# Attention in a decoder trunk: output products of four units in one block, their neighbours' work dealt to three slots of four, and a third PSUM bank for turned exponentials

## The chip, the cores and the metric

The program runs on one core of a Trainium2 chip. The metric is the device time of one execution in microseconds; the kernel before takes 1901.03 us (median of three runs, 1900.66 to 1902.24). TensorE is PE (its weight loads are PEld), VectorE is DVE, ScalarE is ACT, GpSimd is POOL; SP issues most transfers.

## The reference

The trunk has four feed-forward layers (SwiGLU), one short convolution and one attention layer, on 512 tokens of width 1024. Only the attention layer is touched. It is sparse attention in three branches that share 16 heads in 4 groups; with 512 tokens, 8 blocks to select from and 16 selected, the selected branch reads every key, and the window of 512 does so too. Cut to what matters:

```python
s = einsum(q, k) * scale + rel_bias[bucket(dist)]     # per head; k of the selected or of the window branch
p = masked_softmax(s, dist >= 0)
o_branch = einsum(p, v)
out = g0 * o_compressed + g1 * o_selected + g2 * o_window
y = out @ w_out                                       # o is (512, 1024): 16 heads of 64
```

The compressed branch has the same form with 31 compressed keys.

## The kernel before

All large products are in fp32r with operands split into a high and a low part (three matmuls for one, lines 167 to 169). Attention is done by *units*: one unit is one head of one branch with 512 keys (32 units: 4 groups, in each two pairs of heads, in each pair branch 0 for both heads and then branch 1 for both). A unit's work has four stages:

- **logits** (L1277, tile s): eight matmuls in three pieces c = 0, 1, 2, each into a PSUM bank of the tag "s". DVE adds the bias table and takes the smallest (L1287), ACT takes exponentials with their sum (L1296).
- **scaled** (L1302 to L1307): DVE takes reciprocals of the sums, POOL multiplies the unit's exponentials by gate over sum, four instructions.
- **turn** (L1316, tile pt): ten transposes on PE, in three pieces, each into a bank of the tag "t"; ACT copies pieces 0 and 2 to SBUF, DVE piece 1 (L1321, L1322).
- **apply** (L1336, tile o): the turned exponentials times the values, for two heads at once, one into the upper and one into the lower 64 partitions of one bank. The second branch's call adds the compressed branch (L1341, tile o<-pcp,vz), and then ACT and DVE split the finished bank into ohi and olo (L163, L164).

A loop runs over slots v. Slot v issues the logits of unit v+3, scales unit v+2, turns unit v+1, and in every odd slot, behind the third piece, applies units v-1 and v; I call one such call a *block*. Around them a slot takes *pieces* of other work (fill): projections of the next group's queries (twelve matmuls a piece, tile nat, L167 to L169), turning of its heads and keys (tile pk, L1164, followed by DVE at L1182 and L1191), the compressed branch's logits (tile pc, L1231, with DVE at L1235 and L1238, and pct), and the output projection of finished groups (tile y). `share` deals a list of steps to slots by weights; `places` fixes others to a slot. The eight PSUM banks are four pairs: "nat" for nat, pc, pct, pk and y alike, "s" for logits, "t" for turned pieces and "o" for outputs; a pair's banks are taken in turn, in the order of the program text.

The order on each engine is fixed when the program is built: a scheduler takes the instructions by readiness and by the order of the program text, with `issue_after` as a constraint, and each engine then works through its list in that order.

Of the kernel before, what the change touches and what calls it, by code (L numbers as in the profile page):

```python
# [13 lines left out]
F32 = mybir.dt.float32  # L14
F32R = mybir.dt.float32r
# [7 lines left out]
P = 128  # L23
D = 1024
T = 512
# [28 lines left out]
def decoder_kernel(ctx, tc, xT, cT, ng, adaw, adab, ffi, ffo, cwi, cw, cwo,  # L54
# [3 lines left out]
    def pool(es, name, bufs, **kw):  # L58
        kw.setdefault("reuse_waits", "tile")
        return es.enter_context(tc.tile_pool(name=name, bufs=bufs, **kw))  # L60
# [8 lines left out]
    tp = pool(ctx, "tp", 1)  # L69
# [3 lines left out]
    ps = pool(ctx, "ps", 1, space=PSUM)  # L73
    six = cycle(("nat", "s", "t"))


    def psum(name, tag="mm"):
        tag = next(six) if tag == "mm" else {"pr": "o"}.get(tag, tag)
        return ps.tile([P, T], F32, name=name, tag=tag, bufs=2)


    TAGS = {"t": (4, T), "sq": (2, T), "xr": (2, HT), "dg": (1, T)}
# [32 lines left out]


    cbs = [psum("cb", "nat") for c in range(D // T)]
    for c, o in enumerate(cbs):
        nc.tensor.matmul(o, ones[0:1], crow[:, c * T:(c + 1) * T], start=True, stop=True)
# [42 lines left out]
    def split(src, hi, lo):  # L162
        act = nc.scalar.activation(hi, src, AF.Copy)  # L163
        return act, nc.vector.tensor_tensor(lo, src, hi, ALU.subtract)  # L164
# [735 lines left out]
    def nsa(s, nrm, nxt, w0, ahead):  # L900
        with ExitStack() as es:
            na = pool(es, "na", 1, side="right")
            hpool = es.enter_context(ExitStack())
# [11 lines left out]
            kn = [[t[:, :, b] for t in kt] for b in range(2)]  # L915
            vn = [[na.tile([P, NG, HD], F32, name=f"vn{b}{t}") for t in range(NB)] for b in range(2)]
            kc = na.tile([P, NG, 2, NPAD], F32R, name="kc")
            vcc = na.tile([P, HD], F32, name="vcc")
            gsb = na.tile([P, NB, 48], F32, name="gsb")
# [51 lines left out]
            def values_and_gates(dst, own):  # L971
                n = CW + 48
                w = [weights(nwv[:, k:min(k + 3, KD)], min(3, KD - k), n, own if k == 3 else None, 2 if k == 3 else 3)
                     for k in range(0, KD, 3)]
                ge = tmp("ge", NB * 48).rearrange("p (a b) -> p a b", a=NB)

                def quarter(t):
                    o = psum("nat")
                    tk = slice(t * P, (t + 1) * P)
                    for k in range(KD):  # L980
                        wh, wl = w[k // 3]
                        mm3(o[:, 0:n], h[0][k][:, tk], h[1][k][:, tk], wh[:, k % 3, :], wl[:, k % 3, :], k == 0, k == KD - 1)
                    nc.vector.tensor_copy(dst[t], o[:, 0:CW].rearrange("p (g e) -> p g e", e=HD))
                    nc.scalar.activation(ge[:, t, :], o[:, CW:n], AF.Exp, scale=-1.0)
                    if t == NB - 1:
                        nc.vector.tensor_scalar(ge, ge, 1.0, None, op0=ALU.add)
                        nc.vector.reciprocal(gsb, ge)

                return quarter
# [41 lines left out]
            K = [[na.tile([P, T], F32R, name=f"k{b}{e}") for e in range(2)] for b in range(2)]  # L1031
            Q = [na.tile([P, T], F32R, name=f"q{q}") for q in range(NG)]
            keys, spread_keys, heads = turners(qn, kt, K, Q)
# [5 lines left out]
            with ExitStack() as es2:  # L1039
# [21 lines left out]
                v1 = values_and_gates(vn[1], nw)  # L1061
# [8 lines left out]
                v1(3)  # L1070
                for b in range(2):
                    spread_keys(b)
            return attend(es, s, nxt, ahead, K, Q, keys, spread_keys, heads, vn, kc, vcc, gsb, query_steps, value_steps, last_weight, hpool)


    def compressor(es, os, kc, vcc):
# [118 lines left out]

    LOFF = {3: 0, 2: 512, 0: 896, 1: 1024}

    def attend(nsa_es, s, nxt, ahead, K, Q, keys, spread_keys, heads, vn, kc, vcc, gsb, query_steps, value_steps, last_weight, hpool):
        oh, ol = [], []
        ow = pool(nsa_es, "ow", 8, side="right")  # L1200
        units = [(g, 2 * pr + e, b) for g in range(NG) for pr in range(2) for b in range(2) for e in range(2)]
        half = [slice(0, HD), slice(HD, P)]
        with ExitStack() as es:
            at = pool(es, "at", 1)
# [60 lines left out]
            Ls, sts, pts, os, last_turn, last_out = {}, {}, {}, {}, [], []  # L1265
# [43 lines left out]
            def turn(u, c):  # L1309
                pt = psum("pt", "t")  # L1310
                off, segs = 0, []
                for j in ((0,), (1, 3), (2,))[c]:
                    segs.append((j, off))
                    for i in range(j, NB):
                        cc = LOFF[i] + j * P
                        last_turn[:] = [nc.tensor.transpose(pt[:, off:off + P], Ls[u][:, cc:cc + P], ident)]  # L1316
                        off += P
                p = at.tile([P, off], F32, name=f"p{c}", bufs=3)
                pts[u, c] = p, segs
                if c == 1:  # L1320
                    return lambda: nc.vector.tensor_copy(p, pt[:, 0:off])  # L1321
                nc.scalar.activation(p, pt[:, 0:off], AF.Copy)  # L1322
                return lambda: None

            def apply(u):

                g, q, b = units[u]
                if b == 0:
                    os[g, q // 2] = psum("o", "o")
                o = os[g, q // 2]  # L1330
                for c in range(3):
                    both = [pts.pop((u + e, c)) for e in range(2)]
                    for j, cc in both[0][1]:
                        n = T - j * P
                        for e in range(2):
                            last = nc.tensor.matmul(o[half[e], j * P:T], vn[b][j][:, g], both[e][0][:, cc:cc + n],  # L1336
                                                    start=(b == 0 and j == 0), stop=False)
                if b == 0:
                    return last
                for e in range(2):  # L1340
                    last = nc.tensor.matmul(o[half[e]], vz[:, q + e], pcp, start=False, stop=True)  # L1341
                del os[g, q // 2]
                hi, lo = [(tp if g % 2 else ow).tile([P, T], F32R, name=n, tag="t", bufs=4 if g % 2 else 8) for n in ("ohi", "olo")]
                split(o, hi, lo)
                oh.append(hi)
                ol.append(lo)
                return last
# [19 lines left out]
            for g in range(NG):  # L1367
                v0 = 8 * g
# [17 lines left out]
            def share(v):  # L1386
                for steps, n, v0, v1 in shares:
                    if v0 <= v < v1:
                        room = [2 - (i > 0 and i % 2) for i in range(v0, v1)]
                        upto_ = [n * sum(room[:i]) // sum(room) for i in (v - v0, v - v0 + 1)]  # L1390
                        return steps, upto_[1] - upto_[0], v == v1 - 1
                return None, 0, False

            for v in range(START, N):
                a, b, u = v + LEAD, v + 1, v
                steps, n, end = share(v)

                def fill(c):
                    for f in places[v, c]:
                        f()  # L1400
                    for _ in range(n * (c + 1) // 3 - n * c // 3):
                        next(steps, None)

                for c in range(3):
                    if 0 <= a < N:
                        sps = logits(a, c)
                    if c == 0 and 0 <= a - 1 < N:
                        scaled(a - 1)
                    if 0 <= b < N:
                        low = turn(b, c)  # L1410
                    if u % 2 and 0 < u and c == 2:
                        with tc.issue_after(last_turn[0].ins):
                            last_out[:] = [apply(u - 1)]
                    if 0 <= a < N:
                        smallest(a, c, sps)
                    if 0 <= b < N:
                        low()
                    if 0 <= a < N:
                        exponentials(a, c)
                    with tc.issue_after(last_out[0].ins) if last_out and c == 2 else nullcontext():  # L1420
                        fill(c)
                for g, q in tables[v]:
                    table(g, q)
                if end:
                    for _ in steps:
                        pass
        w0 = ahead()
        for a, b in HALVES:
            for d in range(KD):
                o = psum("ty")  # L1430
# [36 lines left out]
    nxt = Norm(1)  # L1467
    soon = upto(1)
    w = ffn(0, 0, nrm, nxt, None, conv_ahead, [small] + late(2, -1), soon)
    nrm, nxt = nxt, Norm(2)  # L1470
# [4 lines left out]
    nrm, nxt = nxt, Norm(3)  # L1475
    w = ffn(2, 1, nrm, nxt, w, ffn_ahead(2), late(5, -3))
    nrm, nxt = nxt, Norm(4)
    w = ffn(3, 2, nrm, nxt, w, lambda: nsa_in(4), late(6))
    cd_es.close()
    nrm, nxt = nxt, Norm(5)  # L1480
    w = nsa(4, nrm, nxt, w, ffn_ahead(3))
    ffn(5, 3, nxt, None, w, None)

# [73 lines left out]
```

## Time and profile before

| what | value |
|---|---|
| median of 3 runs | 1901.03 us |
| the profiled execution's own time | 1900.09 us |
| its span | 1898.3 us |
| PE busy in the span | 1872.5 us, 99% |
| attention slots, first logits to last output product | 1323.9 to 1533.2 us |
| PE, DVE, ACT, POOL busy in these 209.3 us | 203.4, 161.0, 133.8, 80.5 us |

The page of the profile gives busy time by engine, the span in 40 slices, and the chain of work that ended last. The timeline lists instructions of one engine in order with start and duration; "x16" merges sixteen of a kind. A matmul's duration is its latency in the pipeline, so the distance between two starts says what it costs, not the duration. An fp32 product such as o appears twice in the trace (two passes) for one row of the program.

### The profile page before, as it was taken

To read this page: it belongs to the slowest core of one execution; us is meant where nothing else is said; L and a number is where in the kernel's file an instruction comes from. 1 tells how busy PE (TensorE), PEld (TensorE's weight loads), DVE (VectorE), ACT (ScalarE), POOL (GpSimd) and SP (SyncE) were. 2 spreads that over 40 slices of the span, in tenths; PEclk is the share of its full clock that TensorE was granted. 3 is DMA by queue.
4 is the path that set the end of the run, shared out by engine and by line. 5 is a ranking of instruction groups with operands and counts; after the bars stand their busy time and mean duration, and the time that the engine had idled before them with its cause. 6 is when DMAs were issued, how large, how long until landed. Compare 5 with 4: busy or idle time off the path is not lost.

```text
span 1898.3 us, 33954 instructions
## 1 busy us (share of the span) xinstructions
PE 1872.5 (99%) x13293; PEld 1710.8 (90%) x13293; DVE 1562.9 (82%) x2671; ACT 857.5 (45%) x1399; POOL 225.5 (12%) x330
## 2 busy tenths in 40 slices
PE   7999999999999999999999999999999999999999
PEld 5989999988899899999989899999777789898989
DVE  8978888887898888888888888887878778586865
ACT  3434344532245343435634343454666636353432
POOL 0011110000011111100111110000444310010100
PEclk9999999999999999999999999999999999999999
DMA  9587767366756767664667766234333235474731
GB/s 330 176 257 188 244 178 229 116 231 232 254 151 183 229 182 244 180 218 114 172 222 189 225 176 215 70 114 128 87 97 84 69 87 152 140 190 125 187 110 64
DMA packets 126669, 324.60 MB, mean 171 GB/s; under 512 B 16011, under 2 KB 16651, under 8 KB 126508
## 3 DMA queue, kind: packets, MB, share of 16 engines
q1 hardware_dynamic: 95196, 242.72, 37.8%
q0 software_dynamic: 31312, 79.71, 18.5%
q8 instruction: 104, 1.70, 0.4%
q14 instruction: 57, 0.47, 0.1%
HBM read 313.85 MB, written 3.15 MB: 167 GB/s over the span
## 4 chain that ended last, share of the span: by engine, by line
PE 87%; DVE 9%; ACT 2%; issue 1%; DMA 1%; DVEq 0%; ACTq 0%
PE gu L169 13%; PE gu L167 13%; PE gu L168 13%; PE y L167 7%; PE y L169 7%; PE y L168 7%; PE hs L168 2%; PE hs L169 2%; PE hs L167 2%; PE cv L167 2%; PE cv L169 2%; PE cv L168 2%; PE o L1336 2%; PE ty L168 2%; PE ty L169 2%; PE ty L167 2%
## 5 line engine op out<-in xcount | busy, mean ns | idle before, releaser
L163 ACT ACTIVATE whi<-wraw 128x1024 fp32r<-128x1024 f32 (+2 forms) x261 | 254.4, 979 | 370.6 <-PE y L168 205.3
L164 DVE TENSOR_TENSOR wlo<-wraw,whi 128x1024 fp32r<-128x1024 f32 (+2 forms) x261 | 295.2, 1136 | 24.2 <-ACT whi L163 23.2
L167 PE MATMUL y<-ahi,whi 128*128 128x512 f32 x576 | 223.7, 392 | 1.0
L168 PE MATMUL y<-alo,whi 128*128 128x512 f32 x576 | 224.3, 389 | 0.0
L169 PE MATMUL y<-ahi,wlo 128*128 128x512 f32 x576 | 224.2, 389 | 0.0
L147 DVE CUSTOM_DVE_ANT_0 adaraw<-adaraw,cond,adabs 128x1024 f32<-128x1024 f32 x144 | 184.4, 1297 | 27.9 <-DMA adaraw<-in_adaw 27.7
L167 PE MATMUL gu<-hhi,whi 128*128 128x256 f32 x696 | 192.5, 277 | 0.0
L169 PE MATMUL gu<-hhi,wlo 128*128 128x256 f32 x696 | 192.4, 276 | 0.0
L168 PE MATMUL gu<-hlo,whi 128*128 128x256 f32 x696 | 192.4, 276 | 0.0
L655 POOL DMA_DIRECT2D qa<-in_ffi x70 | 84.4, 1206 | 711.7 <-DMA qa<-in_ffi 197.2
L167 PE MATMUL gu<-th,qah 128*128 128x256 f32 x584 | 161.3, 276 | 0.0
L168 PE MATMUL gu<-tl,qah 128*128 128x256 f32 x584 | 161.2, 276 | 0.0
L169 PE MATMUL gu<-th,qal 128*128 128x256 f32 x584 | 161.2, 276 | 0.0
L167 PE MATMUL gu<-th,qbh 128*128 128x256 f32 x584 | 161.2, 276 | 0.0
L168 PE MATMUL gu<-tl,qbh 128*128 128x256 f32 x584 | 161.2, 276 | 0.0
L169 PE MATMUL gu<-th,qbl 128*128 128x256 f32 x584 | 161.2, 276 | 0.0
L167 PEld LDWEIGHTS y<-ahi,whi 128*128 128x128 f32 x576 | 107.2, 188 | 26.9 <-ACT ahi L163 5.7
L167 PEld LDWEIGHTS gu<-hhi,whi 128*128 128x128 f32 x696 | 130.7, 188 | 0.5
L168 PEld LDWEIGHTS gu<-hlo,whi 128*128 128x128 f32 x696 | 130.6, 188 | 0.5
L169 PEld LDWEIGHTS gu<-hhi,wlo 128*128 128x128 f32 x696 | 130.7, 188 | 0.0
L169 PEld LDWEIGHTS y<-ahi,wlo 128*128 128x128 f32 x576 | 108.1, 188 | 22.7
L168 PEld LDWEIGHTS y<-alo,whi 128*128 128x128 f32 x576 | 108.1, 188 | 22.3
(312 smaller groups left out, 5379.6 us busy)
## 6 DMA issues: line engine op xcount, KB each, us to landing
wraw<-in_ffi SPq DMA_DIRECT2D x103, 512.0 KB
adaraw<-in_adaw POOLq DMA_DIRECT2D x79, 512.0 KB, 4.4
qa<-in_ffi SPq DMA_DIRECT2D x146, 256.0 KB
wraw<-in_ffo SPq DMA_DIRECT2D x96, 384.0 KB
qa<-in_ffi POOLq DMA_DIRECT2D x70, 512.0 KB, 6.9
adaraw<-in_adaw SPq DMA_DIRECT2D x65, 512.0 KB
a<-in_ffi SPq DMA_DIRECT2D x73, 256.0 KB
wraw<-in_cwi SPq DMA_DIRECT2D x24, 512.0 KB
```

The source lines that it names most:

```text
L147: return nc.vector.tensor_tensor_reduce(out=raw, in0=raw, in1=cond, scale=scale, scalar=adabs[:, c:c + 1], op0=ALU.mult, op1=ALU.add, accu ...
L163: act = nc.scalar.activation(hi, src, AF.Copy)
L164: return act, nc.vector.tensor_tensor(lo, src, hi, ALU.subtract)
L167: nc.tensor.matmul(o, sh, mh, start=first, stop=False)
L168: nc.tensor.matmul(o, sh, ml, start=False, stop=False)
L169: nc.tensor.matmul(o, sl, mh, start=False, stop=last)
L655: nc.gpsimd.dma_start(qa, bass.AP(tensor=a21.tensor, offset=a21.offset, ap=[a21.ap[0], [0, 2], a21.ap[1]]), accum_op=ALU.add)
L1336: last = nc.tensor.matmul(o[half[e], j * P:T], vn[b][j][:, g], both[e][0][:, cc:cc + n], start=(b == 0 and j == 0), stop=False)
```

## The change

Five things are edited, all in or for `attend`:

- Blocks: in every fourth slot (u % 4 == 3), ahead of piece 1's logits, both branches of a pair of heads are applied one behind the other (`apply(u - 3)`, `apply(u - 1)`), in place of one in every odd slot behind piece 2. Pieces in front of them are constrained by `issue_after` in piece 1 in place of piece 2.
- Dealing: `share` gives weight 1 to the slots without a block and 0 to those with one (before: 2 and 1).
- Banks: within attention the tag "t" rotates over three banks and "o" has one; outside, each tag has two as before.
- Copies: the turned exponentials have 5, 4 and 4 buffers in place of 3 each.
- Room: the pool "ow" has 4 buffers in place of 8; group 2's outputs go to the space of the tiles kn.

```diff
+    banks = {t: cycle((t + "0", t + "1")) for t in ("nat", "s", "t", "o")}
+
     def psum(name, tag="mm"):
         tag = next(six) if tag == "mm" else {"pr": "o"}.get(tag, tag)
-        return ps.tile([P, T], F32, name=name, tag=tag, bufs=2)
+        return ps.tile([P, T], F32, name=name, tag=next(banks[tag]), bufs=1)
...
-        ow = pool(nsa_es, "ow", 8, side="right")
+        ow = pool(nsa_es, "ow", 4, side="right")
+        kept = dict(banks)
+        banks["t"], banks["o"] = cycle(("t0", "t1", "o1")), cycle(("o0",))
...
-                p = at.tile([P, off], F32, name=f"p{c}", bufs=3)
+                p = at.tile([P, off], F32, name=f"p{c}", bufs=(5, 4, 4)[c])
...
-                hi, lo = [(tp if g % 2 else ow).tile([P, T], F32R, name=n, tag="t", bufs=4 if g % 2 else 8) for n in ("ohi", "olo")]
+                if g == 2:
+                    two = na.tile([P, 2, T], F32R, name="o2", tag=f"kn{q // 2}")
+                    hi, lo = two[:, 0], two[:, 1]
+                else:
+                    hi, lo = [(tp if g else ow).tile([P, T], F32R, name=n, tag="t", bufs=4) for n in ("ohi", "olo")]
...
-                        room = [2 - (i > 0 and i % 2) for i in range(v0, v1)]
+                        room = [i < 0 or i % 4 < 3 for i in range(v0, v1)]
...
                 for c in range(3):
+                    if u % 4 == 3 and 0 < u and c == 1:
+                        with tc.issue_after(last_turn[0].ins):
+                            apply(u - 3)
+                            last_out[:] = [apply(u - 1)]
                     if 0 <= a < N:
                         sps = logits(a, c)
                     if c == 0 and 0 <= a - 1 < N:
                         scaled(a - 1)
                     if 0 <= b < N:
                         low = turn(b, c)
-                    if u % 2 and 0 < u and c == 2:
-                        with tc.issue_after(last_turn[0].ins):
-                            last_out[:] = [apply(u - 1)]
...
-                    with tc.issue_after(last_out[0].ins) if last_out and c == 2 else nullcontext():
+                    with tc.issue_after(last_out[0].ins) if last_out and c == 1 else nullcontext():
                         fill(c)
...
+        banks.update(kept)
```

Every engine has the same instructions as before; their order changes between the first logits and the end of attention. (Line numbers of the change are 2 to 10 higher than those of before from line 78 on: L1320 is the transpose L1316, L1340 the product L1336, L1281 the logits L1277, L1166 the transposes of heads and keys L1164, L169 to L171 the three matmuls L167 to L169.)

The first place is PE's list in the opening of attention, where the second group's queries are projected (nat) beside the first units' logits (s) and transposes (pt). Before, a stretch of it:

```order
L1277 MATMUL s<-k_13505,q_13510 128x512
L1277 MATMUL s<-k_13506,q_13510 128x512
L168 MATMUL nat<-wlo,hhi_13485 128x256
L169 MATMUL nat<-whi,hlo_13489 128x256
L167 MATMUL nat<-whi,hhi_13485 128x256
L168 MATMUL nat<-wlo,hhi_13485 128x256
L169 MATMUL nat<-whi,hlo_13489 128x256
L1277 MATMUL s<-k_13505,q_13510 128x384
L1277 MATMUL s<-k_13506,q_13510 128x384
L1277 MATMUL s<-k_13505,q_13510 128x128
```

Of the change, the end of the same stretch:

```order
L1281 MATMUL s<-k_13505,q_13512 128x512
L1281 MATMUL s<-k_13506,q_13512 128x512
L1320 MATMUL pt<-ident,L 128x128 x6
L1281 MATMUL s<-k_13505,q_13512 128x384
L1281 MATMUL s<-k_13506,q_13512 128x384
L1281 MATMUL s<-k_13505,q_13512 128x128
L1281 MATMUL s<-k_13506,q_13512 128x128
L1320 MATMUL pt<-ident,L 128x128 x11
L1340 MATMUL o<-p_14945,vn_13494 64x512
L169 MATMUL nat<-whi,hhi_13484 128x256
L170 MATMUL nat<-wlo,hhi_13484 128x256
L171 MATMUL nat<-whi,hlo_13488 128x256
```

Before, 84 of the 96 matmuls nat of this projection stand between logits and transposes of the first five units, ahead of the first block; now all 96 stand behind the last transpose x11 and the first row of the first block. (The compressed branch's two pieces pc now take both banks of "nat" ahead of this projection, which so waits for DVE's reads at L1235 and L1238; before, the projection's first half had the second bank.)

The second place is PE's list at the end of the first pair of heads, in slot 3. Before, from the last rows of the second block:

```order
L1336 MATMUL o<-p_15161,vn_13500 64x256
L1336 MATMUL o<-p_15263,vn_13500 64x256
L1341 MATMUL o<-pcp,vz 64x512
L1164 MATMUL pk<-ident,qn_14873 128x128 x2
L1164 MATMUL pk<-ident,qn_14874 128x128 x2
L1341 MATMUL o<-pcp,vz 64x512
L1277 MATMUL s<-k_13507,q_13512 128x512
```

And now, from the middle of the one block:

```order
L1340 MATMUL o<-p_15005,vn_13496 64x256
L1340 MATMUL o<-p_15071,vn_13496 64x256
L1340 MATMUL o<-p_15123,vn_13498 64x512
L1340 MATMUL o<-p_15203,vn_13498 64x512
L1340 MATMUL o<-p_15137,vn_13499 64x384
L1340 MATMUL o<-p_15221,vn_13499 64x384
L1340 MATMUL o<-p_15137,vn_13501 64x128
L1340 MATMUL o<-p_15221,vn_13501 64x128
L1340 MATMUL o<-p_15161,vn_13500 64x256
L1340 MATMUL o<-p_15254,vn_13500 64x256
L1345 MATMUL o<-pcp,vz 64x512 x2
L1281 MATMUL s<-k_13507,q_13511 128x384
```

The two branches now follow each other without other rows in between, and nothing stands between the two rows of vz. Over the whole of attention the rows of o stood in 22 runs (16 blocks, of which four were broken up by other rows, two of them into three runs) and stand in 11 now (8 blocks, three of which have their first row alone, ahead of other rows).

More of the change, by code (lines that the diff above doesn't have):

```diff
@@ L1072, in nsa @@
                     spread_keys(b)
-            return attend(es, s, nxt, ahead, K, Q, keys, spread_keys, heads, vn, kc, vcc, gsb, query_steps, value_steps, last_weight, hpool)
+            return attend(es, na, s, nxt, ahead, K, Q, keys, spread_keys, heads, vn, kc, vcc, gsb, query_steps, value_steps, last_weight, hpool)
     def compressor(es, os, kc, vcc):
@@ L1196, in decoder_kernel, with attend @@
     LOFF = {3: 0, 2: 512, 0: 896, 1: 1024}
-    def attend(nsa_es, s, nxt, ahead, K, Q, keys, spread_keys, heads, vn, kc, vcc, gsb, query_steps, value_steps, last_weight, hpool):
+    def attend(nsa_es, na, s, nxt, ahead, K, Q, keys, spread_keys, heads, vn, kc, vcc, gsb, query_steps, value_steps, last_weight, hpool):
         oh, ol = [], []
-        ow = pool(nsa_es, "ow", 8, side="right")
+        ow = pool(nsa_es, "ow", 4, side="right")
+        kept = dict(banks)
+        banks["t"], banks["o"] = cycle(("t0", "t1", "o1")), cycle(("o0",))
         units = [(g, 2 * pr + e, b) for g in range(NG) for pr in range(2) for b in range(2) for e in range(2)]
```

## The prediction

> **What bounds the kernel now.** First the page:
>
> ```profile
> span 1898.3 us, 33954 instructions
> PE 1872.5 (99%) x13293; PEld 1710.8 (90%) x13293; DVE 1562.9 (82%) x2671; ACT 857.5 (45%) x1399; POOL 225.5 (12%) x330
> ...
> PE   7999999999999999999999999999999999999999
> ...
> PE 87%; DVE 9%; ACT 2%; issue 1%; DMA 1%; DVEq 0%; ACTq 0%
> ```
>
> PE is busy in every slice and carries 87% of the chain that ended last, so whatever the change is worth must come out of PE's time in the attention slots (slices 28 to 32 of 40). Behind them PE is as full as ahead of them, so a gain or a loss there reaches the end at its whole size. Then the attention slots, cut where units 2, 6, 10, 14, 18 and 22 begin their logits (columns: length, then busy time of each engine):
>
> ```profile
> 1331.90:1353.70 21.80, 21.12 (x163) 18.00 (x161) 17.03 (x55) 14.66 (x42) 9.46 (x20) 1.00 0.32 87
> 1353.70:1381.00 27.30, 26.33 (x177) 19.37 (x178) 20.81 (x64) 17.90 (x51) 10.95 (x20) 1.00 0.40 104
> 1381.00:1404.00 23.00, 22.52 (x171) 17.99 (x169) 18.10 (x58) 16.00 (x44) 10.00 (x20) 1.00 0.30 86
> 1454.50:1481.40 26.90, 25.22 (x155) 17.86 (x155) 22.61 (x67) 17.64 (x50) 11.88 (x20) 1.00 0.37 85
> sum 209.30, PE 203.37 PEld 155.43 DVE 161.02 ACT 133.78 POOL 80.45; mean PE 22.60 PEld 17.27 DVE 17.89 ACT 14.86 POOL 8.94
> ```
>
> Four units cost 23 us in one stretch and 27 in the next: the long ones turn the next group's heads and keys, where DVE has most to do (20.8 and 22.6 us). PE's idle time in all is only 209.30 - 203.37 = 5.9 us. Who ends it, by the waits of PE in these slots:
>
> ```profile
> PE pt L1316 <- ACT p L1322: 2.2, 4, 0.7
> PE s L1277 <- DVE st L1287: 1.2, 4, 0.3
> PE pt L1316 <- DVE p L1321: 0.5, 1, 0.5
> ```
>
> So 2.7 us are transposes that wait for one of two banks to be copied out. The rest of what can be won is not idle time at all, and the timeline of PE shows it, at two blocks that stand whole:
>
> ```profile
> 1363.55 0.84 PE L1316 MATMUL pt<-ident,L 128*128 128x128 f32 x6
> 1364.14 0.37 PE L167 MATMUL nat<-whi,hhi 128*128 128x256 f32 x1
> ...
> 1396.72 0.48 PE L1277 MATMUL s<-k,q 128*128 128x256 f32 x2
> 1397.04 0.38 PE L1316 MATMUL pt<-ident,L 128*128 128x128 f32 x2
> 1397.35 2.37 PE L1336 MATMUL o<-p,vn 128*64 128x512 f32 x16
> 1399.66 0.39 PE L167 MATMUL nat<-whi,hhi 128*128 128x256 f32 x1
> 1399.88 0.28 PE L168 MATMUL nat<-wlo,hhi 128*128 128x256 f32 x1
> 1400.00 0.28 PE L169 MATMUL nat<-whi,hlo 128*128 128x256 f32 x1
> ...
> 1407.20 2.37 PE L1336 MATMUL o<-p,vn 128*64 128x512 f32 x16
> 1409.40 1.03 PE L1341 MATMUL o<-pcp,vz 128*64 128x512 f32 x4
> 1410.36 0.73 PE L1277 MATMUL s<-k,q 128*128 128x512 f32 x2
> ```
>
> Read the distances between starts. Six transposes take 0.59 us to the next start, 0.10 each; the two ahead of a block take 0.31, so going into it costs 0.11. The block's sixteen passes take 2.31 us where nat follows and 2.20 where its own vz follows: going out costs 0.11, and the first nat behind it takes 0.22 instead of the 0.12 of the next, 0.10 more. **An edge pair costs 0.32 us**, and none of it is counted idle. Blocks that other rows break up are dearer:
>
> ```profile
> 1358.53 1.02 PE L1341 MATMUL o<-pcp,vz 128*64 128x512 f32 x2
> 1359.61 0.44 PE L1164 MATMUL pk<-ident,qn 128*128 128x128 f32 x2
> ...
> 1360.58 1.07 PE L1341 MATMUL o<-pcp,vz 128*64 128x512 f32 x2
> 1361.58 0.73 PE L1277 MATMUL s<-k,q 128*128 128x512 f32 x2
> ...
> 1417.31 1.07 PE L1336 MATMUL o<-p,vn 128*64 128x512 f32 x2
> 1418.31 0.68 PE L1277 MATMUL s<-k,q 128*128 128x512 f32 x2
> ...
> 1420.77 2.37 PE L1336 MATMUL o<-p,vn 128*64 128x512 f32 x14
> 1423.07 0.39 PE L167 MATMUL nat<-whi,hhi 128*128 128x256 f32 x1
> ```
>
> Two rows of vz side by side cost 0.96 us (1409.40 to 1410.36), apart 1.08 + 1.00: **1.1 us more**. A first row of o alone and its fourteen passes later cost 1.00 + 2.30, against 2.31: **1.0 more**. The two heads' rows, in different halves of the array, run side by side only when neighbours.
>
> **The change part by part.** *Edges.* Blocks fall from 16 to 8. One of those saved lies in the opening, which I cost whole below; 7 x 0.32 = -2.2 us.
>
> *Broken blocks.* Before, slots 3 and 13 have the two breaks shown, slots 5 and 21 one each with three runs, taken at 1.1 like the first: 1.1 + 1.0 + 2 x 1.1 = 4.3. Now three blocks have their first row alone, 3 x 1.0 = 3.0. -1.3 us. (Bounds: 0, if a lone row's cost is hidden in a wait, and -2.4, if the three cost a third of that.)
>
> *Alternation.* With pieces gathered in fewer slots, changes from fp32r products (s, nat, y) into transposes fall from 95 to 82. The two s rows at 1396.72 take 0.32 us to the next start where two nat rows take 0.23: at most 0.09 for each change; bounds 0 and -1.2, taken in the middle near nothing, -0.5.
>
> *The opening.* Before, 84 rows of nat fill PE while the first units go through DVE, ACT and POOL; now they come later, and PE waits on that chain. Its pace, by POOL:
>
> ```profile
> 1328.88 0.20 POOL L1304 TENSOR_TENSOR f<-r,gsb 128x4 f32<-128x4 f32 x1 [15.79 <-DVE r L1302]
> 1329.19 2.05 POOL L1307 TENSOR_SCALAR L<-L,f 128x128 f32<-128x128 f32 x4
> 1332.38 0.20 POOL L1304 TENSOR_TENSOR f<-r,gsb 128x4 f32<-128x4 f32 x1 [1.14 <-DVE r L1302]
> ...
> 1342.62 0.28 PE L167 MATMUL nat<-whi,hhi 128*128 128x256 f32 x1
> 1346.26 0.28 PE L169 MATMUL nat<-whi,hlo 128*128 128x256 f32 x1
> ...
> 1353.64 0.73 PE L1277 MATMUL s<-k,q 128*128 128x512 f32 x2 [0.31 <-DVE st L1287]
> ```
>
> The first two units are 3.5 us apart. The transposes x11 need unit 4 scaled: 1328.9 + 4 x 3.3 (a little under 3.5, since no nat stands between) + 2.4 for POOL = 1344.5. Then 96 nat at (1346.26 - 1342.62)/32 = 0.114 make 10.9, four pct 0.4, the first row of o 0.45 without its break: unit 6 begins at 1356.3 instead of 1353.6. By then the change has also done some 0.9 us less of PE's work (seven rows of o fewer, 7/8 of 2.20 = 1.9, against seven transposes and the rest more). Together **+3.6 us**. At a pace of 3.0 (POOL is busy 2.4 a unit, so there is room) it is +2.4, at 3.5 +4.4. The cover, were it there, would be any other PE work ready in that time; the list has none.
>
> *The third bank and the copies.* Transposes no longer wait for the copy of two pieces back: at best the 2.7 us of the waits above go. At worst, logits wait more: their banks are still two, and during a block of 2.20 + 2.20 + 0.96 = 5.4 us no logits come, then all at once. Behind the block in slot 3 stand, on PE, pk and the next logits; on DVE, olo, then L1287, L1191 and L1182 in one list; POOL's scaling waits for those, and the next transposes for POOL. Against that DVE has a projection's normalisation and a weight split to do under the block. Bounds -5.9 (all idle time) and +7.5 (rival C); taken near the row for the transposes, less 0.5 for logits: -2.2.
>
> *Nothing.* `ow`, kn's space and the order of transfers: SP's list differs by a few places, and no wait of PE in the rows above is on a transfer. ACT and POOL have 209.3 - 133.8 and more to spare; what covers them is PE itself.
>
> Sum: -2.2 - 1.3 - 0.5 + 3.6 - 2.2 = **-2.6 us** on the span, 1895.7. The profiled execution took 1900.1 for a span of 1898.3, and the median lies 0.9 above it: 1895.7 + 1.8 + 0.9 = **1898.4 us**.
>
> **The rivals.** *B, the waits go with the edges* (chance 0.20). With PE free of short stalls all 5.9 us of idle time go, and the opening runs at 3.0 a unit: -2.2 - 1.3 - 0.5 + 2.4 - 5.9 = -7.5, 1893.5 us. For it: 2.7 of 5.9 are exactly what a third bank removes. Against: the rest waits for DVE and other banks. [...]
>
> *C, the long block starves DVE* (0.18): slower. A block holds PE 5.4 us at a stretch instead of 2.3 and 3.2, so DVE is without logits for some 2.5 us longer; in the three stretches with heads and keys, where DVE needs 20.8 to 22.6 us and PE's own work is not much more, that time comes back as PE's waits: 3 x 2.5 = +7.5 in place of -2.2. Sum +7.1, 1908.1 us. It decides where the DVE work left at a block's end is longer than PE's up to the next one. For it: L1287 waits for PE already. Against: DVE was idle 6.5 us in 27.3 there, and waits that fall under a block cost nothing. [...] The trace shows so far that the stretch with more DVE work is the longer one, 27 against 23 us.
>
> *D, the gain and the opening cancel* (0.20). The transposes' waits turn into waits for logits, none saved: -0.4 and less, 1900.6 to 1904. The change then does what it says and PE is only idle elsewhere.
>
> **How the numbers follow.** The forecast, 1898.4, has 0.42; its own range is 1895.5 to 1900.5. Bounds of the unknown terms give 1893.5 to 1908; the range that leaves out less than two in ten is 1891.5 to 1906. A measurement of this kernel tells about 0.2%, 3.8 us, from no change: faster means below 1897.2, which takes B and 0.18 of the forecast, 0.38; slower, above 1904.8, is C, 0.18; the rest, 0.44, is no difference.
>
> **What would show it.** Edges: the sum of L1336's time should fall while its count stays; two blocks back to back in 5.4 us. Opening: unit 6's logits about 2.7 us later after the first logits than now, PE idle about 4 us before the first row of nat. Bank: no PE wait of pt for ACT's copy; if those stay, the third bank was not the limit. C would show as PE's waits of s for DVE growing from 1.2 us to several in the stretches of heads and keys. I am wrong about the opening if PE is not idle there, and about the edges if the 27 us stretches do not shrink.

## The result: slower by 0.7%

The changed kernel takes 1914.73 us (median of six, 1913.27 to 1917.77), beside it the kernel before 1900.99: ratio 1.0072, interval 1.0061 to 1.0083. Forecast were 1898.4 us and at most 1906.0. The profiled execution took 1917.77 us, the longest of the six, so its losses are some 3 us above those of the median. Its page:

```profile
span 1916.0 us, 33925 instructions
PE 1879.0 (98%) x13293; PEld 1719.7 (90%) x13293; DVE 1564.9 (82%) x2671; ACT 857.0 (45%) x1399; POOL 223.5 (12%) x330
...
PE 83%; DVE 7%; issue 5%; POOL 2%; ACT 1%; DMA 1%; SPq 0%; DVEq 0%; POOLq 0%; ACTq 0%
```

POOL, with 12% of busy time, is new in the chain that ended last. The span is 17.7 us longer. Of this 1.7 is, in the main, a wait for a weight (y for wlo, 1.6) at 522 us, long ahead of the change (the other traces show none there or up to 0.5 us); 0.9 lies just ahead of the first logits, 0.9 behind attention, and 14.2 in attention itself: 223.2 us from the first logits to the last output product, before 209.0. The stretches that begin with the logits of units 2, 6, 10 and 22, and the sum over attention (columns as before; behind POOL stands the granted clock of TensorE, 1.00 being full speed):

```profile
1334.90:1362.80 27.90, 25.41 (x175) 20.79 (x174) 16.60 (x54) 15.80 (x46) 8.99 (x20) 0.98 0.29 89
1362.80:1390.00 27.20, 24.86 (x169) 20.38 (x167) 22.42 (x66) 18.08 (x49) 9.06 (x20) 0.94 0.42 110
1390.00:1412.90 22.90, 22.61 (x170) 18.42 (x169) 16.81 (x56) 15.62 (x43) 9.18 (x20) 1.00 0.17 42
1465.70:1495.60 29.90, 26.56 (x156) 20.14 (x155) 25.32 (x66) 18.94 (x50) 11.54 (x23) 0.94 0.50 136
...
sum 223.20, PE 209.06 PEld 163.45 DVE 162.51 ACT 134.31 POOL 78.64; mean PE 23.23 PEld 18.16 DVE 18.06 ACT 14.92 POOL 8.74
```

PE's idle time rose from 5.9 to 14.1 us, and its busy time rose by 6.0 with the same instructions. DVE, ACT and POOL have no more to do than before. The opening up to unit 6 takes 36.3 us in place of 29.8; the stretch from 22 to 26 takes 29.9 in place of 26.9.

**Who ends the idle time.** The waits of PE in attention:

```profile
PE pt L1320 <- POOL L L1311: 7.9, 18, 1.2
PE y L169 <- DVE q L1193: 2.0, 1, 2.0
PE s L1281 <- DVE st L1291: 0.9, 4, 0.3
PE pk L1166 <- DVE q L1193: 0.8, 1, 0.8
PE pt L1320 <- DVE p L1325: 0.3, 1, 0.3
```

(Each row: what waited, for whom; us in total, number of waits, the longest.) The waits for ACT's copies are gone, as the third bank was to do. In their place transposes wait for POOL's scaling, 18 times; before, no wait of PE for POOL stood in this list. More of the same hides in PE's busy time: adding the distances from one start to the next over all 320 transposes, without idle time, gives 41.9 us in place of 35.0. They come one or two at a time as POOL finishes a row block, and their weight loads wait for POOL 34 times, before twice:

```profile
PEld pt L1320 <- POOL L L1311: 16.5, 34, 1.3
```

**Where the wait begins.** PE behind the first block, that of slot 3:

```profile
1368.60 0.79 PE L1281 MATMUL s<-k,q 128*128 128x384 f32 x4
...
1373.65 0.66 PE L1166 MATMUL pk<-ident,qn 128*128 128x128 f32 x4 [0.77 <-DVE q L1193]
1374.11 1.11 PE L1281 MATMUL s<-k,q 128*128 128x384 f32 x6
1376.22 1.70 PE L1320 MATMUL pt<-ident,L 128*128 128x128 f32 x4 [1.00 <-POOL L L1311]
...
1379.60 0.56 PE L169 MATMUL nat<-whi,hhi 128*128 128x256 f32 x1
```

DVE in the same time:

```profile
1367.73 1.29 DVE L960 TENSOR_TENSOR qn<-qn,rs_r 128x512 f32<-128x512 f32 x2
1368.94 1.22 DVE L166 TENSOR_TENSOR wlo<-wraw,whi 128x1024 fp32r<-128x1024 f32 x1
1370.07 0.69 DVE L166 TENSOR_TENSOR olo<-o,ohi 128x512 fp32r<-128x512 f32 x1
1370.67 0.55 DVE L1291 CUSTOM_DVE_ANT_0 L<-s,tb 128x384 f32<-128x384 f32 x1
...
1375.25 0.16 DVE L1306 RECIPROCAL r<-st 128x4 f32<-128x4 f32 x1
```

And POOL:

```profile
1365.16 2.09 POOL L1311 TENSOR_SCALAR L<-L,f 128x128 f32<-128x128 f32 x4
1375.49 0.20 POOL L1308 TENSOR_TENSOR f<-r,gsb 128x4 f32<-128x4 f32 x1 [8.24 <-DVE r L1306]
1375.79 2.05 POOL L1311 TENSOR_SCALAR L<-L,f 128x128 f32<-128x128 f32 x4
```

Of before, the same scaling:

```profile
1368.91 0.20 POOL L1304 TENSOR_TENSOR f<-r,gsb 128x4 f32<-128x4 f32 x1 [5.33 <-ACT p L1322]
```

In the change the first logits behind the block come at 1368.6, DVE gets to them at 1370.7, the reciprocals are there at 1375.4, POOL, idle for 8.2 us, begins at 1375.5 and the transposes at 1376.2. That chain is no longer than before: there the logits behind the same products stood at 1361.6 and POOL began at 1368.9, 7.3 us against 6.9. What is missing is PE's work beside it. Before, twenty transposes, twelve nat and the next block's first row, with logits and pk, filled that time; now thirteen transposes, logits and pk stand there, the block has run whole ahead of it, and the first nat comes at 1379.6.

**The clock.** PE's other loss is one that the prediction doesn't mention at all. Windows of 3.41 us in pairs, the second of each just where the records show half clock:

```profile
1328.95:1332.36 3.41, 2.24 (x15) 2.04 (x15) 1.82 (x10) 2.28 (x8) 0.73 (x3) 1.00 0.28 69
1332.36:1335.77 3.41, 3.36 (x13) 2.72 (x14) 1.86 (x9) 2.68 (x9) 1.52 (x3) 0.50 0.21 35
1373.33:1376.74 3.41, 1.97 (x12) 1.54 (x12) 3.38 (x13) 2.67 (x9) 1.15 (x4) 1.00 0.62 160
1376.74:1380.15 3.41, 3.30 (x13) 2.81 (x14) 1.40 (x4) 1.64 (x7) 1.10 (x2) 0.50 0.68 151
...
1475.72:1479.13 3.41, 1.45 (x13) 1.21 (x11) 3.35 (x7) 3.18 (x9) 0.00 (x0) 1.00 0.66 167
1479.13:1482.54 3.41, 3.41 (x10) 2.72 (x11) 3.22 (x10) 1.10 (x4) 2.25 (x5) 0.50 0.74 166
```

Four times in attention a window in which PE is busy for 1.45 to 2.24 of 3.41 us (0.42 to 0.66) is followed by one at clock 0.50 (the one not printed begins at 1427.93, behind one with 1.83 us); the kernel before has none in attention. At clock 0.50 four transposes take 0.70 us to the next start (1378.15 to 1378.85), at 1.00 they take 0.38 (1398.07 to 1398.45). Four windows at half clock are by estimate up to 4 x 3.41 / 2 = 6.8 us of PE's work lost, and each sits right behind a wait for POOL or DVE, of 1.16, 1.00, 0.99 and 1.96 us: these waits are paid twice. The clock is not the whole of it: the mean granted clock was 0.996 in the execution of 1917.77 us and 0.999 in that of 1913.27, which by this mean had about one such window and still lies 12.3 us above before.

**What the blocks gave.** A whole block of four:

```profile
1392.12 4.53 PE L1340 MATMUL o<-p,vn 128*64 128x512 f32 x32
1396.48 1.03 PE L1345 MATMUL o<-pcp,vz 128*64 128x512 f32 x4
1397.44 0.79 PE L1281 MATMUL s<-k,q 128*128 128x384 f32 x4
```

5.32 us from first to last start (4.36 and 0.96). All rows of o and vz together take 45.5 us from start to start, before 48.1: 2.6 are won. The account of attention: idle +8.2, half clock +6.8, transposes at full clock +4.2 (6.9 less the 2.7 that they lost at half clock), o -2.6, all other rows together -2.4 (what is left over): +14.2.

### The profile page after: what moved, and what is told of

The parts are those of the page before. It is cut to its first block, busy times and chain, and to the rows that moved or that the text cites. A ratio compares the mean times of both kernels' runs of the same rounds, so it can differ in the third digit from the quotient of the medians.

```text
span 1916.0 us, 33925 instructions
## 1 busy us (share of the span) xinstructions
PE 1879.0 (98%) x13293; PEld 1719.7 (90%) x13293; DVE 1564.9 (82%) x2671; ACT 857.0 (45%) x1399; POOL 223.5 (12%) x330
## 4 chain that ended last, share of the span: by engine, by line
PE 83%; DVE 7%; issue 5%; POOL 2%; ACT 1%; DMA 1%; SPq 0%; DVEq 0%; POOLq 0%; ACTq 0%
PE gu L169 13%; PE gu L171 13%; PE gu L170 13%; PE y L169 7%; PE y L170 6%; PE y L171 6%; POOL L L1311 2%; PE cv L169 2%; PE cv L171 2%; PE cv L170 2%; PE hs L170 2%; PE hs L169 2%; PE hs L171 2%; PE ty L170 2%; PE ty L171 2%
## 5 line engine op out<-in xcount | busy, mean ns | idle before, releaser
L169 PE MATMUL y<-ahi,whi 128*128 128x512 f32 x576 | 223.6, 391 | 1.0
L171 PE MATMUL y<-ahi,wlo 128*128 128x512 f32 x576 | 224.1, 389 | 0.0
L169 PE MATMUL gu<-hhi,whi 128*128 128x256 f32 x696 | 192.5, 277 | 0.0
L171 PE MATMUL gu<-hhi,wlo 128*128 128x256 f32 x696 | 192.4, 276 | 0.0
L169 PE MATMUL gu<-th,qah 128*128 128x256 f32 x584 | 161.4, 276 | 0.0
L171 PE MATMUL gu<-th,qal 128*128 128x256 f32 x584 | 161.2, 276 | 0.0
L169 PE MATMUL gu<-th,qbh 128*128 128x256 f32 x584 | 161.2, 276 | 0.0
L171 PE MATMUL gu<-th,qbl 128*128 128x256 f32 x584 | 161.2, 276 | 0.0
L169 PEld LDWEIGHTS y<-ahi,whi 128*128 128x128 f32 x576 | 107.3, 188 | 27.1 <-ACT ahi L165 5.7
L169 PEld LDWEIGHTS gu<-hhi,whi 128*128 128x128 f32 x696 | 130.7, 188 | 0.5
L171 PEld LDWEIGHTS gu<-hhi,wlo 128*128 128x128 f32 x696 | 130.7, 188 | 0.0
L171 PEld LDWEIGHTS y<-ahi,wlo 128*128 128x128 f32 x576 | 108.1, 188 | 22.5
```

The costliest lines, as they stand in the source:

```text
L169: nc.tensor.matmul(o, sh, mh, start=first, stop=False)
L171: nc.tensor.matmul(o, sl, mh, start=False, stop=last)
```

## The experiments

Two theories stood against each other. *Starved chain*: a block of four lets no logits through and takes PE's cover out of the following gap, so that DVE, ACT and POOL are late. *Dealing*: the pieces that covered this were dealt away. Each of the first four runs takes back one part, or all but one. The kernel before takes 1901.5 to 1902.0 us beside the experiments.

**The third bank alone.** Blocks and dealing of before, everything else of the change:

```diff
-room = [i < 0 or i % 4 < 3 for i in range(v0, v1)]
+room = [2 - (i > 0 and i % 2) for i in range(v0, v1)]
-if u % 4 == 3 and 0 < u and c == 1:  apply(u - 3), apply(u - 1)
+if u % 2 and 0 < u and c == 2:  apply(u - 1)     # behind turn(b, c)
...                                              # fill waits for it in piece 2 again
```

> Blocks and dealing as before; of the change only the third bank for turned exponentials (one bank left for outputs), their 5, 4 and 4 copies and the moved room for outputs. If the bank is worth what the waits of before say (2.2 us of transposes that wait for ACT's copy, 0.5 for DVE's): 1898.3 us, and no wait of pt for p. If the single output bank or the rest does harm, as a theory 'the banks cost the time' needs: 1908 to 1915 us, with waits of the first row of o for the split of the bank. If those waits only move to another row: 1901 us. No window of PE at half clock is expected in the last two of these cases unless PE's busy share in one falls to about two thirds.

1903.51 us, ratio 1.0009 (1.0000 to 1.0017): nearest to the case that the waits only move, but with windows of half clock that it left out. No wait for ACT's copies is left, but PE's idle time is 5.4 us against 5.9: the transposes now wait 1.5 us for POOL, the logits 1.7 for DVE. The rows of o are broken up more, into 27 runs that take 49.4 us (before 22 and 48.1). The run shows the price of the clock by itself. Of eleven executions of this one program, four had a granted clock of 1.000 and took 1900.93 to 1902.38 us (mean 1901.5); seven had 0.998 and took 1903.16 to 1906.83 (mean 1904.7). The profiled one is of the latter, with two windows of half clock in a row (of the other six only the mean clock is known):

```profile
1479.70:1483.10 3.40, 2.63 (x14) 1.89 (x15) 2.58 (x11) 2.50 (x10) 2.27 (x5) 0.95 0.39 64
1483.10:1489.97 6.87, 6.87 (x29) 5.41 (x29) 3.74 (x16) 2.88 (x10) 2.27 (x5) 0.53 0.35 138
```

The seven are slower by 3.2 us on the mean (half of 6.8 would be 3.4), and at full clock, 1901.5 us beside 1901.5 for before, the bank is worth nothing.

**The old dealing, blocks of four kept.**

```diff
-room = [i < 0 or i % 4 < 3 for i in range(v0, v1)]
+room = [2 - (i > 0 and i % 2) for i in range(v0, v1)]
```

> The change with the weights of before in the dealing of pieces (2 and 1), blocks of four and the third bank kept. Theory 'block': a block of 5.4 us lets no logits through, behind it the chain logits, DVE, ACT, DVE, POOL takes 8 us, and transposes wait for POOL's scaling whatever the dealing: 1909 to 1915 us, with at least 5 us of waits of pt for POOL. Theory 'dealing': the pieces that covered this were dealt away: 1897 to 1901 us, with under 2 us of such waits and no window at half clock.

1906.78 us, ratio 1.0024 (1.0014 to 1.0035): between the theories, and 8 us below the change.

```profile
PE pt L1320 <- POOL L L1311: 5.9, 14, 1.1
```

Most of the waits for POOL are still there. Behind the block of slot 3 PE reaches the first nat 6.0 us after the logits (1364.0 and 1370.0), in the change 11.0 us.

**Blocks of two, the new dealing and the bank kept.** The second half of the first diff, from the line `if u % 4 == 3` on.

> The change with blocks of two in every odd slot, as before; the third bank and the new dealing kept. Theory 'block': 1898 to 1902 us, waits of pt for POOL under 1 us. Theory 'dealing': 1908 to 1915 us, as the pieces are still missing in every fourth slot and in the opening; waits of pt for POOL of 5 us and more. If both are needed at once: about 1901 to 1904.

1903.28 us, ratio 1.0009 (0.9999 to 1.0018), the same as the bank alone, and in the range for both causes being needed at once. So in all the new dealing does no harm with blocks of two, and 8 us of harm with blocks of four (1914.7 against 1906.8). Over the whole of attention the two causes don't add: the dealing costs only where the block has already taken the cover. (The opening is an exception, below.)

**Two banks each, blocks of four and new dealing kept.**

```diff
-banks["t"], banks["o"] = cycle(("t0", "t1", "o1")), cycle(("o0",))
```

> The change with two banks for turned exponentials and two for outputs, as before; blocks of four and the new dealing kept. If the banks are no part of the loss: 1914 to 1918 us, as the change or up to 2.7 us above it (the waits for copies come back), waits of pt for POOL of 7 us and more, and windows at half clock again. If the single output bank is the cause: 1900 to 1904 us.

1912.52 us, ratio 1.0057 (1.0044 to 1.0069), below the change and not above it.

```profile
PE pt L1320 <- POOL L L1311: 7.5, 13, 1.2
PE s L1281 <- DVE st L1291: 2.6, 5, 1.5
PE pt L1320 <- ACT p L1326: 2.5, 5, 1.0
```

The waits for copies are back, and the time is not: about two windows of half clock fewer, by the mean granted clock of the profiled execution (0.998 in place of 0.996), and two of three lone first rows of a block gone (o takes 43.5 us in place of 45.5).

**The logits of a block's slot ahead of it.** A test of the chain itself: nothing is dealt otherwise, the next unit only enters it before the block holds PE.

```diff
+if block:
+    for c in range(3): smallest(a, c, logits(a, c)); ...; exponentials(a, c)
 for c in range(3):
     if block and c == 1: apply(u - 3), apply(u - 1)
-    sps = logits(a, c)
+    if not block: sps = logits(a, c)
```

> The change with one thing moved: in a slot with a block, all three pieces of the next unit's logits, with DVE's smallest and ACT's exponentials, are written ahead of the block (now one piece ahead, two behind). Theory 'starved chain' (behind the block POOL has no unit to scale, since no logits went through for 5.4 us, and PE's transposes wait for it): DVE and ACT work under the block, the 7.9 us of waits of pt for POOL fall below 4 and windows at half clock fall to two or fewer: 1905 to 1909 us. Rival 'dealing alone' (PE has too little ready work in the slots behind the block, whoever is late): no change, 1912 to 1917 us, the waits only change their names.

1908.16 us, ratio 1.0033 (1.0021 to 1.0046), 6.6 us below the change and in the range of the starved chain, though the waits did not fall below 4:

```profile
PE pt L1320 <- POOL L L1311: 4.4, 9, 1.3
```

The block of slot 3 runs to 1368.5 in this trace, and POOL now scales two units under it in place of one. The second begins here; in the change it came at 1375.5, behind the block:

```profile
1366.97 0.20 POOL L1308 TENSOR_TENSOR f<-r,gsb 128x4 f32<-128x4 f32 x1 [1.03 <-DVE r L1306]
```

The mean granted clock of the profiled execution is 0.999, where the change's is 0.996 with its four windows: by estimate one window of half clock is left. The rival, under which only the names would change, falls.

**Both, logits ahead and old dealing.**

> As the run before (all logits of a block's slot ahead of the block), and the weights of before in the dealing. If the two causes add (5 to 8 us for the dealing, 5 to 8 for the chain) nothing of the loss is left and the edges saved show: 1897 to 1901 us, no window at half clock, waits of pt for POOL under 2 us. If the old dealing had already covered what the logits bring: 1904 to 1908 us, as with the old dealing alone (1906.8).

1903.37 us, ratio 1.0009 (1.0000 to 1.0018); the waits for POOL are 3.4 us. This lies between the two ranges: nearly all of the loss is gone, but no gain shows. Unit 6 still begins 33.6 us behind the first logits, in an execution at a mean clock of 0.999, by estimate one window of half clock; from unit 6 to the end it takes 176.3 us, before 179.2.

**Three of POOL's four scalings left out, in the change and in the kernel before.**

```diff
-for i in range(NB):    # L *= gate / sum, four row blocks
+for i in (1,):
```

> The change with three of POOL's four scalings of a unit left out (the exponentials of three row blocks go unscaled into the transposes): POOL's part of the chain falls from 2.05 us to about 0.5 for a unit. Theory 'starved chain': POOL is the last 2 us of some 8.6 us between the first logits behind a block and their transposes, so each of the waits at the ends of seven blocks and in the opening shrinks by up to 1.5 us and windows at half clock get rarer: 1903 to 1909 us. If POOL itself is too slow (its time for a unit sets the pace): all 7.9 us of waits and the windows go, 1899 to 1903 us. If PE's waits for POOL are no part of the loss: 1913 to 1916 us.

> The kernel before with the same three scalings left out, as a measure of what the cut brings where no transposes wait for POOL: 1900 to 1902 us, under 1 us from before, since no wait of PE for POOL stands in its list. If it gains 3 us and more, the cut shortens something else and the run before says less about the blocks.

The change falls by 12.6 us to 1902.09 (ratio to the uncut kernel before 1.0002, 0.9992 to 1.0011), the kernel before by 2.3 to 1899.71 (0.9990, 0.9981 to 0.9999), a little below the 1900 to 1902 expected. The change's fall is more than I had given to the starved chain and lies in the range of a POOL that is itself too slow, but that case's sign, that all waits for POOL go, did not come; 5.2 us of them are left:

```profile
PE pt L1320 <- POOL L L1311: 5.2, 7, 1.7
```

What I had left out of both cases is the clock. The profiled execution has no window of half clock (mean clock 1.000; up to 6.8 us less), 9.3 us of idle time in place of 14.1, and the transposes take 36.9 us from start to start in place of 41.9. The two runs show that PE's losses hang on when POOL is done: 10.4 us more in the change than before, with an engine that is busy for 79 of 223. For 6.6 us the run with the logits ahead shows that this is the chain's lateness and not POOL's pace, as POOL has as much to do there as ever; how far POOL's own 2.05 us a unit makes up the rest was not taken apart.

**The opening.** First the change with blocks of two and the old weights up to slot 3; then with the old weights alone.

```diff
+room = [2 - (i > 0 and i % 2) if v0 < 3 else i % 4 < 3 for i in range(v0, v1)]
-if u % 4 == 3 and 0 < u and c == 1:
+if u % 4 == 3 and 4 < u and c == 1:       # and u in (1, 3), c == 2: apply(u - 1)
...
```

> The change with its opening put back: up to slot 3 blocks of two in slots 1 and 3 and the old weights for the pieces dealt there; from slot 4 on blocks of four and the new dealing. In the change unit 6 begins 36.3 us behind the first logits, before 29.8. Theory 'the opening is nearly half of the loss': unit 6 begins at 29 to 31, the whole is 6 us below the change's 1914.7, 1907 to 1910 us; the rest, 7 us, is the later starved stretches. If the opening's loss is only taken over by the next stretch: 1912 to 1915.

> The change with only the weights of the opening put back (pieces of the slots below 3 dealt as before); blocks of four from the first one on. If in the opening the dealing is the cause (the projection's 96 matmuls moved behind the first block): unit 6 begins at 30 to 32 us, 1908 to 1911 us. If the block of four alone keeps the opening long: unit 6 at 33 to 36 us, as with the old dealing throughout (34.3), and 1911 to 1915 us.

1910.88 us (1.0048, 1.0036 to 1.0060) with unit 6 at 31.6 us, and 1913.62 us (1.0062, 1.0050 to 1.0074) with unit 6 at 33.6. The opening is worth some 4 us and not 6, between the two ranges of the first of these runs. Block and dealing both count there: unit 6 begins at 31.6 us with neither, at 33.6 with the block of four alone, at 34.4 with the new dealing alone (the run with blocks of two) and at 36.3 with both, so in the opening they do add, 2.0 and 2.8 to 4.7. The change has one window of half clock in its opening (at 1332.36). With the block of four and the old dealing PE is still busy for only 1.46 us of one stretch of 3.41, from 1349.92 on, and the clock in the next stretch of 3.41 us is 0.52.

**The three repairs together, with the third bank and with two banks.**

> All three repairs at once: opening as before (blocks of two up to slot 3), old weights everywhere, and in the slots with a block of four all logits ahead of it. Behind the opening the run with the last two repairs took 176.3 us from unit 6 to the last output, before takes 179.2; with before's 29.8 for the opening this makes 206.1 in place of 209.0: 1898 to 1900 us, about 2.5 below before, and no window at half clock. If what the blocks save is lost again at the seam between opening and blocks of four: 1901 to 1903 us.

> The run with all three repairs, and two banks each for turned exponentials and for outputs, as before: what the third bank is worth once nothing starves. If it is worth the 2.7 us of waits for copies that the trace of before showed: 1901 to 1903 us, waits of pt for ACT's or DVE's copy of p of 2 us and more. If those waits had only stood in for the wait for POOL, which comes at the same rows: 1899 to 1900.5 us, and the bank is worth nothing.

With the third bank 1899.66 us, ratio 0.9989 (0.9980 to 0.9997); with two banks **1896.17 us, ratio 0.9970 (0.9958 to 0.9982)**, below both kernels of this case; neither run has a window of half clock in attention. The second lies below both ranges that I gave it: I had not expected the third bank to cost anything. The copies and the moved room of the change stand in both and were not tried apart. Attention with the third bank, as the windows give it:

```profile
1325.20:1531.30 206.10, 200.49 (x1361) 157.31 (x1360) 160.13 (x478) 132.85 (x366) 81.23 (x160) 1.00 0.30 84
```

and with two:

```profile
1324.30:1526.70 202.40, 196.58 (x1361) 154.09 (x1359) 160.69 (x478) 132.59 (x366) 81.41 (x160) 1.00 0.32 85
```

The idle time is alike (5.6 and 5.8 us); the bank costs PE busy time. The second block of four, with the third bank:

```profile
1403.96 1.07 PE L1340 MATMUL o<-p,vn 128*64 128x512 f32 x2
1404.96 1.07 PE L1281 MATMUL s<-k,q 128*128 128x384 f32 x6
1405.96 3.98 PE L1340 MATMUL o<-p,vn 128*64 128x512 f32 x27
```

and with two banks:

```profile
1403.36 4.53 PE L1340 MATMUL o<-p,vn 128*64 128x512 f32 x32
1407.71 1.03 PE L1345 MATMUL o<-pcp,vz 128*64 128x512 f32 x4
```

A lone first row (two passes) takes 1.00 us, and the 34 passes behind the logits, vz included, take 5.31 to the next start; the whole block takes 5.32, and the logits in between are paid apart, so each such row costs 1.0. With the third bank the rows of o stand in 15 runs and take 47.0 us, with two banks in 11 and take 43.8. That is 3.1 of the 3.7 us between the two in attention. Why the scheduler breaks blocks more readily with the banks dealt this way was not tried.

## Why the prediction was wrong, point by point

**Edges and broken blocks** (-3.5): right in kind. o won 2.6 us with three lone rows, and 4.3 where eleven runs with one lone row were left (48.1 to 43.8); a lone row costs the 1.0 that I read from the trace. The 0.32 of a single edge pair was not measured apart, nor the alternation. My own sign for the edges, that the 27 us stretches shrink, did not come: the three took 27.2, 26.7 and 29.9 us, before 27.3, 26.6 and 26.9. The waits hid there what the rows of o won.

**The opening** (+3.6): right in mechanism, too small. I put the first nat 21 us behind the first logits, at a pace of 3.3 us a unit; it came at 24.5 us, since POOL's units followed each other at 3.95 us (1331.83 to 1347.62 in four steps), the first of them through a window of half clock. I allowed 0.45 for the lone first row, which took 1.00. Unit 6 began at 36.3 us, not 32.4, that is 6.5 later than before and not 2.7.

**The third bank and the copies** (-2.2): the step that failed. I took it near the row of the waits for copies, and those went as said. But transposes wait for POOL as soon as POOL is late, whatever the banks (7.9 us with the third bank, 7.5 with two). The paragraph names this chain (POOL's scaling waits for DVE behind a block, the transposes for POOL) and gives it 0.5 us of the sum. The runs showed in its place, over all of attention with its opening, 7.9 us of waits for POOL, 8.2 us more idle time in all, 4.2 us more for the transposes and up to 6.8 us at half clock; the old dealing brings back 8.0 us, the logits ahead of the block 6.6, both 11.4. I had read POOL's busy time and found it to spare (under *Nothing*); what counts is the time from a unit's logits to its scaled exponentials, some 7 us behind the block of slot 3, against the PE work that stands between the same two points in its list. The trace of before gave a hint, in the waits of PE's weight loads:

```profile
PEld pt L1316 <- POOL L L1307: 1.2, 2, 0.8
```

Twice already the transposes' loads waited for POOL: at these places there was no slack to take away, and the change takes a block of 2.2 to 3.2 us out of each second gap. The bank itself is worth nothing alone, and costs some 2 us in the change and 3.5 in the repaired kernel.

**Rival C** came closest, 1908.1 us with a chance of 0.18. Its block starves the engines behind the logits, as it said. It named the wrong link, though (logits for DVE: 0.9 us, fewer than before), limited it to the stretches with heads and keys, and left dealing out, without which the loss is 5.2 us and not 13.7. It also gave waits under a block as free; here the work that could have run under it had not been admitted. That its price, +7.5, is near the idle time's +8.2 is luck: only 3.9 of these lie in the three stretches.

**Not in any case: the clock.** 1.00 in every stretch of before let me take a PE microsecond as fixed. It did not decide the miss, as the execution at a mean clock of 0.999 shows, which took 1913.27 us. The trace of the change has four windows of 3.41 us at a clock of 0.50 in attention, on one grid: they begin 44.4, 51.2 and 51.2 us apart, 13, 15 and 15 windows. Ahead of none of them was PE idle for a whole window: its longest single wait in attention was 2.0 us, and the windows just ahead, in which it was still busy for 1.45 to 2.24 us, were at full clock.

## What to carry to other kernels

Cover is local: before merging two stretches of work on the bound engine, write down the time that each chain of work through the other engines takes from its first to its last link, and the bound engine's work that stands between these two points in its list; an engine that is busy for a third of the stretch can be the last link, as POOL was here with 79 of 223 us. A block that holds the bound engine should come after the work that feeds the others has been issued (here worth 6.6 us), and a buffer is worth only the wait that isn't followed by another at the same instruction (the third bank alone, at full clock: 1901.5 us beside 1901.5). A wait can be paid twice: four here, of 0.99 to 1.96 us, were each followed by 3.41 us at half clock.

## What was not expected of the hardware

In attention the trace of the change has four places where the clock fell to one half, for one window of 3.41 us each. In the window ahead of each PE was busy for 2.24, 1.97, 1.83 and 1.45 us, by the records. The window on the same grid with the next least, 2.39 us (from 1462.07), was followed by one at full clock (1.00). In the bank alone two windows of half clock follow each other (6.87 us at a clock of 0.53), and with the weights of the opening alone put back a stretch with PE busy for 1.46 of 3.41 us is followed by one at 0.52. The mean granted clock of the profiled executions of the variants lies between 0.996 and 0.999 except in four at 1.000: with the scalings left out, in the change and before, and in the two repaired kernels. One program gives times some 3 us apart (the bank alone: mean 1901.5 at a clock of 1.000 and 1904.7 at 0.998); only one execution of each program was traced, so where the windows lie in the others was not shown. Left open are what decides that the clock falls, and why the repaired kernels still reach unit 6 at 31.4 to 31.6 us and not at 29.8.
